# Two-layer decoder trunk: a fourth Strassen block in the first half of the second MLP product, and final results taken out of PSUM by ScalarE

## The chip, the core and the metric

The program runs on one core of a Trainium2 chip, in one launch. The time is the device time of one execution in microseconds; the kernel before takes 2175.74 us (median of 3 runs, 2175.13 to 2176.91). In the text TensorE is the matrix engine (PE in the rows, its weight loads PEld), VectorE is DVE, ScalarE is ACT, and SyncE (SP) issues most of the DMAs.

## The reference, cut to what matters

The input is 256 tokens of 2048 channels in float32. Layer 0 is a hybrid of a gated convolution and differential attention, layer 1 is forgetting attention; after each comes the part that the change touches, a dense MLP with 8192 hidden channels:

```
def _sqrelu_mlp(h, w1, w2):
    return jnp.square(jax.nn.relu(h @ w1)) @ w2

h = _rmsnorm(x, norm2_g[l])
x = x + _sqrelu_mlp(h, mlp_w1[l], mlp_w2[l])
```

The results must agree with float32 arithmetic. The kernel therefore writes each operand as the sum of a high and a low part in a reduced format (float32r), and each product as three: high by high, high by low, low by high.

## The kernel before, in words

**Splitting.** A weight tile of 1 MB comes in by one DMA on SP's queue (`raw`, 3 buffers). `split_w` (L139 to L148) makes its high part on ScalarE (`wh`, L146) and its low part on VectorE (`wl`, L147); of each there are 3 buffers in a ring, so a tile's cast waits until TensorE is done with the tile three back.

**Order.** A Tile scheduler sets the order in which instructions stand on each engine when the program is built, and adds semaphores. On the chip each engine goes through its queue in that order. `pending` holds generators of small work (attention, norm chunks), which `step` moves on by one piece after a block of matmuls; `late` holds closures that take a result out of PSUM, and `flush` runs them when the next product's first weights have been split.

**One MLP.** `mlp` (L700) goes through 4 groups of 2048 hidden channels. In each group `hidden` (L606) computes eight products of the first weight (`gemm_t`, two weight tiles each, 64 matmuls of 512 columns and 64 of 256), and `take` squares the result and splits it into a `PairS` or a `PairC` by the letter in `KINDS`. Then `gemm_pair` (L639) runs twice, for column blocks n = 0, 1 and n = 2, 3. It is called the first and the second pair here. Each has eight blocks, one for every letter of `KINDS`:

- A block C is eight products of three matmuls of 512 columns (24 matmuls), from one weight tile.
- A block S is Strassen's form with seven products (21 matmuls). VectorE makes four sums of weights first (`T`, L652 to L655), and two tiles are split: `wa` of 1536 columns from `raw`, and `wb` of 2048 from `T`. The first three products (P1, P2, Q3) need `wa`, the last four (Q5, P7, P6, Q4) `wb`.

A pair fills all eight PSUM banks. P1, Q5, P7 and P6 are only written by blocks S. After the block behind the last S they are combined into `E` and added to the residual `xall` (L680 to L689: one ScalarE copy, five VectorE instructions counted as L682, L683, L684 and twice L689). P2, Q3, X and Q4 collect up to the pair's last product, and `final` (L693) takes them out, with one VectorE instruction each that scales the bank and adds it to the residual (L695), when the next pair or the next group has started.

**The turn from layer 0 to layer 1.** In the last group `done` puts the norm chunks of the next layer on `pending`: chunks 0 and 1 behind `E` of the second pair, chunks 2 and 3 behind the last `final`. A chunk transposes a column block of the residual on TensorE (L198) and splits it into high (ScalarE, L135) and low (VectorE, L136). The first projection of layer 1 (`gemm`, L150) needs chunk 0 for its first matmuls.

The tiles `T`, `E` and the hidden blocks' results share the pool `qkv` under the name `qk`, with 2 buffers.

Of the kernel before, what the change touches and what calls it, by code (L numbers as in the profile page):

```python
# [8 lines left out]
F32 = mybir.dt.float32  # L9
F32R = mybir.dt.float32r  # L10
AF = mybir.ActivationFunctionType
# [5 lines left out]
P = 128  # L17
D = 2048
# [8 lines left out]
def trunk_kernel(  # L27
# [54 lines left out]


    pending = []
    late = []

    def flush():

        while late:
            late.pop(0)()  # L90

    def step():

# [56 lines left out]
    def gemm(acts, w, c0, first=False):  # L150

        acc = []
        total = 4 * len(acts)
        i = 0
        for ai, a in enumerate(acts):
            raw = wraw.tile([P, 4, CW], F32, name="raw")
            src = w[a.row:a.row + CW, c0:c0 + CW].rearrange("(k p) n -> p k n", p=P)
            if first and ai == 0:
                for h in range(4):
                    nc.sync.dma_start(raw[:, h, :], src[:, h, :])  # L160
            else:
                nc.sync.dma_start(raw, src)
            wh, wl = split_w(raw, parts=4 if first and ai == 0 else 2 if first else 1)
            if i == 0:
                flush()
# [76 lines left out]
    gw = const.tile([P, KT, 16], F32, name="gw")  # L242
    gws = const.tile([P, GP], F32R, name="gws")

    def setup():
        rows = work.tile([P, 2 * P], F32, name="y")[:, :P]
# [12 lines left out]
        nc.scalar.dma_start(gw, fox_w_in[0, :, 3 * D:3 * D + 16].rearrange("(k p) n -> p k n", p=P))  # L259


        nc.gpsimd.memset(mask, 0.0)
# [162 lines left out]

    def forget_gates(nm):

        wv = gws[:, :KT * 32].rearrange("p (k n) -> p k n", n=32)
        nc.scalar.copy(gws[:, KT * 32:], ones[:, :96])
        nc.scalar.copy(wv[:, :, 0:16], gw)  # L430
# [115 lines left out]
    def gemm_t(acts, w, c0):  # L546


        acc = []
        for c in range(2):  # L550
            raw = wraw.tile([P, 8, 2 * P], F32, name="raw")
            r0 = c * 8 * P
            nc.sync.dma_start(raw, w[r0:r0 + 8 * P, c0:c0 + 2 * P].rearrange("(k p) n -> p k n", p=P))
            wh, wl = split_w(raw, (8, 2 * P))
            if c == 0:
                flush()
                acc += [accp.tile([P, CW], F32, name="acc") for _ in range(2)]
            for h in range(2):
                a = acts[2 * c + h]
                until(lambda: a.left <= 0)  # L560
                for f, k, p in TORDER:
                    fs = slice(f * P, (f + 1) * P)
                    if p == 0:
                        nc.tensor.matmul(  # L564
                            acc[f], wh[:, 4 * h + k, fs], a.both[:, k, :, :].rearrange("p s t -> p (s t)"),
                            start=c + h + k == 0, stop=False)
                    else:
                        nc.tensor.matmul(acc[f][:, 2 * P:], wl[:, 4 * h + k, fs], a.hi[:, k, :], start=False,  # L568
                                         stop=(c, h, k) == (1, 1, 3))
                step()  # L570
        return acc

    KINDS = "SCSCSCCC"

    class PairS:

# [8 lines left out]
            nc.scalar.copy(self.t[:, :, 0, :], f)  # L587
            nc.vector.tensor_tensor(self.t[:, :, 1, :], f, self.t[:, :, 0, :].bitcast(F32), ALU.subtract)

        def part(self, i):  # L590
            return self.t[:, i, 0, :], self.t[:, i, 1, :]

    class PairC:
# [12 lines left out]
    def hidden(nm, w, c0):  # L606

        pairs, half = [], None
        for i, kind in enumerate(KINDS):
            acc = gemm_t(nm.acts, w, c0 + 2 * i * P)  # L610
            if kind == "S":
                p = PairS()
            elif half is not None:
                p, half = PairC(half), None
            elif "C" in KINDS[i + 1:]:
                t = actp.tile([P, 4, 2, 2 * P], F32R, name="act")
                p, half = PairC(t[:, :2]), t[:, 2:]
            else:
                p = PairC(qkv.tile([P, 2, 2, 2 * P], F32R, name="v"))
# [19 lines left out]
    def gemm_pair(pairs, w, r0, n, r2, done):  # L639

        B = {}
        live = set()
        for i, (kind, p) in enumerate(zip(KINDS, pairs)):
# [5 lines left out]
            more = KINDS[i + 1:]  # L649
            if kind == "S":  # L650
                T = qkv.tile([P, 4, CW], F32, name="qk")
                nc.vector.tensor_tensor(  # L652
# [3 lines left out]
                wa, wb = split_w(raw[:, 1:4]), split_w(T)  # L656
            else:
                wa = split_w(raw)
            if i == 0:
                flush()  # L660
# [14 lines left out]
            else:  # L675
                for k in range(2):
                    for bank, t, h in (("P2", 0, 1), ("Q3", 0, 0), ("X", 1, 0), ("Q4", 1, 1)):
                        mul(bank, p.part(k, t), wa, 2 * k + h, not more and k == 1)
            if i == KINDS.rindex("S") + 1:
                E = qkv.tile([P, 4, CW], F32, name="qk")  # L680
                nc.scalar.copy(E[:, 3], B["P1"])
                nc.vector.tensor_tensor(E[:, 2], B["P6"], E[:, 3], ALU.add)  # L682
                nc.vector.tensor_tensor(E[:, 1], B["P7"], E[:, 2], ALU.add)  # L683
                nc.vector.tensor_tensor(  # L684
                    E[:, 0:3:2], B["Q5"].unsqueeze(1).broadcast_to([P, 2, CW]), E[:, 1:3], ALU.subtract)
                for t in (1, 0):
                    x2 = xall[:, n:n + 2, t, :]
                    e = E[:, 2 - 2 * t:4 - 2 * t]
                    nc.vector.scalar_tensor_tensor(x2, e, r2[:, t:t + 1], x2, ALU.mult, ALU.add)  # L689
                done(0)  # L690
            step()

        def final():  # L693
            for bank, m, t in (("P2", n + 1, 0), ("Q3", n, 0), ("X", n, 1), ("Q4", n + 1, 1)):
                nc.vector.scalar_tensor_tensor(  # L695
                    xr[m][:, t, :], B[bank], r2[:, t:t + 1], xr[m][:, t, :], ALU.mult, ALU.add)
                done(1, m, t)
        late.append(final)

    def mlp(nm, l, nxt):  # L700
        ov = out[0].rearrange("(t p) d -> p t d", p=P)
        r2 = None
        for g in range(4):
# [5 lines left out]
            for n in (0, 2):  # L709
                def done(stage, m=None, t=None, n=n, g=g):  # L710
# [10 lines left out]
                gemm_pair(pairs, mlp_w2[l], g * D, n, r2, done)  # L721
        if nxt is None:
            flush()

    def load_x(n):
        if n > 0:
# [69 lines left out]
```

## Time and profile before

| what | value |
|---|---|
| median of 3 runs | 2175.74 us |
| profiled execution | 2178.49 us |
| its span, first to last instruction | 2176.8 us |
| TensorE busy, matmuls | 2166.2 us, 10738 records |
| TensorE weight loads busy | 1818.3 us |
| VectorE busy | 1547.4 us |
| ScalarE busy | 1052.7 us |
| DMA | 412.08 MB, 189 GB/s over the span |

The profiled execution lies 2.75 us above the median, and 1.7 us of its time lie outside the span. Busy time is a sum over the whole span; matmuls overlap in the pipeline, so TensorE's pace is read from the distance between the starts of matmuls and not from the busy time.

### The profile page before, as it was taken

Reading aid. Unit: us, or ns where it says so; the run is one execution under the profiler, and the core shown is the slowest. Engines: PE = TensorE matmul, PEld = TensorE weight load, DVE = VectorE, ACT = ScalarE, POOL = GpSimd, SP = SyncE. Lnnn points to the kernel's source line nnn. Section 1 sums busy time; section 2 is a strip of 40 time slices with the busy share of each in tenths; the row PEclk is TensorE's granted clock in tenths of the full one; section 3 lists DMA queues with packets and bytes.
Section 4 is the critical chain, followed back from the end, with each engine's and each line's share of the span. In section 5 each row is a group of like instructions: output and inputs, shape, how many; then the busy total and the mean of one; then the engine's idle time right before and its main releaser. Section 6 shows DMA issues by size and latency. Waiting matters only on the chain. (4 is left out here: it accounts for less than half of the span.)

```text
span 2176.8 us, 26071 instructions
## 1 busy us (share of the span) xinstructions
PE 2166.2 (100%) x10738; PEld 1818.3 (84%) x10738; DVE 1547.4 (71%) x1574; ACT 1052.7 (48%) x1101; POOL 19.1 (1%) x17
## 2 busy tenths in 40 slices
PE   9999999999999999999999999999999999999999
PEld 7887888888888888888888888888888888888887
DVE  5666655778769768767855565567787697687687
ACT  6455443544444444445554454445444444444453
POOL 0000000000000000000000000000000000000000
PEclk9999999999999999999999999999999999999999
DMA  8544556555665665665645555555566656656654
GB/s 272 180 159 158 187 177 200 178 167 198 220 193 170 220 193 182 211 189 190 210 163 194 187 183 173 185 166 176 168 207 216 193 174 216 190 191 207 186 192 151
DMA packets 245273, 412.08 MB, mean 189 GB/s; under 512 B 9399, under 2 KB 144802, under 8 KB 245154
## 3 DMA queue, kind: packets, MB, share of 16 engines
q1 hardware_dynamic: 237296, 405.84, 57.6%
q10 hardware_dynamic: 7858, 4.58, 0.7%
q8 instruction: 84, 1.38, 0.3%
q14 instruction: 35, 0.29, 0.0%
HBM read 408.28 MB, written 2.11 MB: 189 GB/s over the span
## 5 line engine op out<-in xcount | busy, mean ns | idle before, releaser
L147 DVE TENSOR_TENSOR wl<-raw,wh 128x2048 fp32r<-128x2048 f32 (+3 forms) x390 | 855.7, 2196 | 476.8 <-ACT wh L146 476.3
L146 ACT CAST wh<-raw 128x2048 fp32r<-128x2048 f32 (+3 forms) x390 | 713.6, 1832 | 654.3 <-PE acc L179 232.0
L564 PE MATMUL acc<-act,wh 128*128 128x512 f32 x2048 | 643.8, 396 | 0.0
L179 PE MATMUL acc<-wh,act 128*128 128x512 f32 x2048 | 565.0, 397 | 0.1
L568 PEld LDWEIGHTS acc<-act,wl 128*128 128x128 f32 x2048 | 384.7, 188 | 90.7
L179 PEld LDWEIGHTS acc<-wh,act 128*128 128x128 f32 x2048 | 376.5, 188 | 75.3 <-issue 2.0
L568 PE MATMUL acc<-act,wl 128*128 128x256 f32 x2048 | 402.4, 278 | 0.0
L179 PE MATMUL acc<-wl,act 128*128 128x512 f32 x1024 | 318.8, 391 | 0.3 <-DVE wl L147 0.3
L564 PEld LDWEIGHTS acc<-act,wh 128*128 128x128 f32 x2048 | 312.3, 189 | 0.8
L636 PE MATMUL acc<-wl,act 128*128 128x512 f32 x656 | 256.1, 390 | 2.1 <-DVE wl L147 1.9
L637 PE MATMUL acc<-wh,act 128*128 128x512 f32 x656 | 255.3, 389 | 0.0
L635 PE MATMUL acc<-wh,act 128*128 128x512 f32 x656 | 251.5, 389 | 0.0
L179 PEld LDWEIGHTS acc<-wl,act 128*128 128x128 f32 x1024 | 192.1, 188 | 42.8 <-issue 0.7
L636 PEld LDWEIGHTS acc<-wl,act 128*128 128x128 f32 x656 | 123.1, 188 | 30.7 <-DVE wl L147 5.2
L635 PEld LDWEIGHTS acc<-wh,act 128*128 128x128 f32 x656 | 123.1, 188 | 25.7
L637 PEld LDWEIGHTS acc<-wh,act 128*128 128x128 f32 x656 | 123.2, 188 | 25.3
L146 ACT CAST wh<-qk 128x2048 fp32r<-128x2048 f32 x48 | 91.8, 1913 | 92.9 <-DVE qk L655 68.7
L147 DVE TENSOR_TENSOR wl<-qk,wh 128x2048 fp32r<-128x2048 f32 x48 | 109.9, 2290 | 22.2 <-ACT wh L146 21.6
L626 ACT COPY qk<-acc 128x256 f32<-128x256 f32 x128 | 47.1, 368 | 132.4 <-PE acc L568 132.4
L635 PE MATMUL tp<-wh,act 128*128 128x512 f32 x192 | 74.7, 389 | 0.0
L636 PE MATMUL tp<-wl,act 128*128 128x512 f32 x192 | 74.7, 389 | 0.0
L637 PE MATMUL tp<-wh,act 128*128 128x512 f32 x192 | 74.7, 389 | 0.0
(173 smaller groups left out, 1434.4 us busy)
## 6 DMA issues: line engine op xcount, KB each, us to landing
raw<-in_mlp_w_dram SPq DMA_DIRECT2D x256, 1024.0 KB, 5.5
raw<-in_fox_w_in_dram SPq DMA_DIRECT2D x48, 1024.0 KB, 5.2
raw<-in_hyb_w_in_dram SPq DMA_DIRECT2D x47, 1024.0 KB, 5.2
raw<-in_hyb_w_out_dram SPq DMA_DIRECT2D x16, 1024.0 KB, 5.2
raw<-in_fox_w_out_dram SPq DMA_DIRECT2D x16, 1024.0 KB, 5.1
ob<-fcd ACTq DMA_DIRECT2D x4, 512.0 KB, 4.5
xr<-in_x_dram SPq DMA_DIRECT2D x3, 512.0 KB, 7.4
raw<-in_hyb_w_in_dram SPq DMA_DIRECT2D x4, 256.0 KB, 4.5
```

The lines of the kernel that those rows point to most:

```text
L146: nc.scalar.copy(wh[:, s], src[:, s])
L147: nc.vector.tensor_tensor(wl[:, s], src[:, s], wh[:, s].bitcast(F32), ALU.subtract)
L179: nc.tensor.matmul(acc[t], x, (wl if p == 1 else wh)[:, k, :], start=st, stop=sp)
L564: nc.tensor.matmul(acc[f], wh[:, 4 * h + k, fs], a.both[:, k, :, :].rearrange("p s t -> p (s t)"), start=c + h + k == 0, stop=False)
L568: nc.tensor.matmul(acc[f][:, 2 * P:], wl[:, 4 * h + k, fs], a.hi[:, k, :], start=False, stop=(c, h, k) == (1, 1, 3))
L626: nc.scalar.copy(fj, acc[j][:, 2 * P:])
L635: nc.tensor.matmul(acc, a[0], b[0], start=not started, stop=False)
L636: nc.tensor.matmul(acc, a[0], b[1], start=False, stop=False)
L637: nc.tensor.matmul(acc, a[1], b[0], start=False, stop=last)
```

## The change

- `KINDS` now holds a row of letters for each pair. The first pair (n = 0) goes from S C S C S C C C to S C S S C S C C, the second (n = 2) to S C S C C S C C. The hidden block with index 3 is stored as a `PairS`, and in the second pair it is used as a C, by way of `part(k, t)`.
- `E` is now combined at `kinds.rindex("S") + 2`, the last block of a pair, behind the split of that block's weights and ahead of its products; before, it stood behind the products of the block with index `rindex("S") + 1`.
- `final` now has two halves. ScalarE takes the four banks into a tile `F` of the `qk` ring, scaled (L713); a single VectorE addition of 2048 columns (L717) adds `F` to the residual. The addition waits in a second list, `later`, and is flushed when the second weight tile of what follows has been split. The last pair of layer 1 keeps the old form (`tail`).
- The small weight of the forget gates (`gw`) and its split (`gws`) lose their own buffers. `gw` is loaded in `forget_gates`, into a tile `y`, and the split goes into a tile of the `act` ring.

The core of the diff:

```diff
-    KINDS = "SCSCSCCC"
+    KINDS = {0: "SCSSCSCC", 2: "SCSCCSCC"}
...
-        def part(self, i):
+        def part(self, i, t=None):
+            i = i if t is None else 2 * i + t
             return self.t[:, i, 0, :], self.t[:, i, 1, :]
...
-            elif "C" in KINDS[i + 1:]:
+            elif i < 3:
                 t = actp.tile([P, 4, 2, 2 * P], F32R, name="act")
                 p, half = PairC(t[:, :2]), t[:, 2:]
             else:
                 p = PairC(qkv.tile([P, 2, 2, 2 * P], F32R, name="v"))
...
-            if i == KINDS.rindex("S") + 1:
+            if i == 1:
+                flush(later)
+            if i == kinds.rindex("S") + 2:
                 E = qkv.tile([P, 4, CW], F32, name="qk")
                 nc.scalar.copy(E[:, 3], B["P1"])
...
                 done(0)
+            if i == 0:
+                flush(late)
...
         def final():
-            for bank, m, t in (("P2", n + 1, 0), ("Q3", n, 0), ("X", n, 1), ("Q4", n + 1, 1)):
-                nc.vector.scalar_tensor_tensor(
-                    xr[m][:, t, :], B[bank], r2[:, t:t + 1], xr[m][:, t, :], ALU.mult, ALU.add)
-                done(1, m, t)
+            if tail:
...
+                return
+            F = qkv.tile([P, 4, CW], F32, name="qk")
+            for bank, j in (("P2", 2), ("Q3", 0), ("X", 1), ("Q4", 3)):
+                nc.scalar.activation(F[:, j], B[bank], AF.Copy, scale=r2[:, j % 2:j % 2 + 1])
+
+            def add():
+                x4 = xall[:, n:n + 2].rearrange("p m t n -> p (m t) n")
+                nc.vector.tensor_tensor(x4, x4, F, ALU.add)
+                for j in range(4):
+                    done(1, n + j // 2, j % 2)
+            later.append(add)
         late.append(final)
...
     def forget_gates(nm):
 
+        gt = actp.tile([P, 16 * P], F32R, name="act")
+        gws = gt[:, :GP]
+        gw = work.tile([P, 2 * P], F32, name="y").rearrange("p (k n) -> p k n", n=16)
+        nc.scalar.dma_start(gw, fox_w_in[0, :, 3 * D:3 * D + 16].rearrange("(k p) n -> p k n", p=P))
+        yield
```

In the order listings below a row is one instruction (or several equal ones): its line, operation, output tile and inputs, and the output's shape. Line numbers of the changed kernel are higher: the weight sums L652, L654, L655 are L661, L663, L664 there; `E` is L673, L674, L675 and L680; the products L635 to L637 are L643 to L645.

VectorE where the second pair starts, before. The first row is the last bank of `E`; the rows L695 are the old `final`.

```order
L684 TENSOR_TENSOR qk<-tp,qk 128x2x512
L652 TENSOR_TENSOR qk<-raw 128x1024
L689 SCALAR_TENSOR_TENSOR xr<-qk,r_3711,xr 128x2x512 x2
L654 TENSOR_TENSOR qk<-qk,raw 128x512
L147 TENSOR_TENSOR wl<-raw,wh 128x1536
L655 TENSOR_TENSOR qk<-qk,raw 128x512
L652 TENSOR_TENSOR qk<-raw 128x1024
L654 TENSOR_TENSOR qk<-qk,raw 128x512
L695 SCALAR_TENSOR_TENSOR xr<-acc,r_3711,xr 128x512
L147 TENSOR_TENSOR wl<-qk,wh 128x2048
L695 SCALAR_TENSOR_TENSOR xr<-acc,r_3711,xr 128x512 x3
L147 TENSOR_TENSOR wl<-raw,wh 128x2048
```

And now:

```order
L147 TENSOR_TENSOR wl<-raw,wh 128x2048
L673 TENSOR_TENSOR qk<-tp,qk 128x512
L147 TENSOR_TENSOR wl<-raw,wh 128x2048
L674 TENSOR_TENSOR qk<-tp,qk 128x512
L661 TENSOR_TENSOR qk<-raw 128x1024
L675 TENSOR_TENSOR qk<-tp,qk 128x2x512
L663 TENSOR_TENSOR qk<-qk,raw 128x512
L680 SCALAR_TENSOR_TENSOR xr<-qk,r_3712,xr 128x2x512 x2
L664 TENSOR_TENSOR qk<-qk,raw 128x512
L147 TENSOR_TENSOR wl<-raw,wh 128x1536
L147 TENSOR_TENSOR wl<-qk,wh 128x2048
L717 TENSOR_TENSOR xr<-xr,qk 128x2048
```

The first row now is the low part for the first pair's block with index 6, and the second L147 that for index 7. All of `E` stands between these and the second pair's first weights, and behind L717 comes the low part for the second pair's block with index 1.

ScalarE at the same place, before: the high parts for index 7 of the first pair and 0 of the second, and then on.

```order
L681 COPY qk<-tp 128x512
L146 CAST wh<-raw 128x2048 x2
L146 CAST wh<-raw 128x1536
L146 CAST wh<-qk 128x2048
L146 CAST wh<-raw 128x2048
```

And now:

```order
L672 COPY qk<-tp 128x512
L146 CAST wh<-raw 128x2048
L146 CAST wh<-raw 128x1536
L713 ACTIVATE qk<-acc,r_3712 128x512
L146 CAST wh<-qk 128x2048
L713 ACTIVATE qk<-acc,r_3712 128x512 x3
L146 CAST wh<-raw 128x2048
L146 CAST wh<-raw 128x1536
```

The first bank is taken out ahead of the high part of the second pair's `T`, the other three ahead of the high part for index 1.

TensorE in the second pair now, from the first matmul that uses the weights of index 1 (wh_5312, wl_5313). Five matmuls need only high parts, the sixth is the first that needs the low part; wh_5347 belongs to index 2.

```order
L643 MATMUL acc_5281<-wh_5312,act_4448 128x512
L643 MATMUL acc_5282<-wh_5312,act_4448 128x512
L643 MATMUL acc_5284<-wh_5312,act_4448 128x512
L643 MATMUL acc_5283<-wh_5312,act_4448 128x512
L643 MATMUL tp_5285<-wh_5347,act_4535 128x512
L644 MATMUL acc_5281<-wl_5313,act_4448 128x512
L645 MATMUL acc_5281<-wh_5312,act_4448 128x512
```

The scheduler draws high-by-high matmuls forward in the same way inside index 0 (four of them, ahead of the first that needs the low part of `T`) and in index 2.

VectorE at the turn to layer 1, before. L136 are low parts of the next layer's norm chunks.

```order
L684 TENSOR_TENSOR qk<-tp,qk 128x2x512
L689 SCALAR_TENSOR_TENSOR xr<-qk,r_3711,xr 128x2x512 x2
L136 SCALAR_TENSOR_TENSOR act<-tp,g_95,act 128x256 x2
L147 TENSOR_TENSOR wl<-raw,wh 128x2048 x2
L136 SCALAR_TENSOR_TENSOR act<-tp,g_95,act 128x256 x2
L695 SCALAR_TENSOR_TENSOR xr<-acc,r_3711,xr 128x512 x4
L147 TENSOR_TENSOR wl<-raw,wh 128x2048
L136 SCALAR_TENSOR_TENSOR act<-tp,g_95,act 128x256 x4
```

And now:

```order
L675 TENSOR_TENSOR qk<-tp,qk 128x2x512
L680 SCALAR_TENSOR_TENSOR xr<-qk,r_3712,xr 128x2x512 x2
L147 TENSOR_TENSOR wl<-raw,wh 128x2048
L717 TENSOR_TENSOR xr<-xr,qk 128x2048
L136 SCALAR_TENSOR_TENSOR act<-tp,g_95,act 128x256 x4
L147 TENSOR_TENSOR wl<-raw,wh 128x2048
```

Before, the four low parts of chunk 0 stood ahead of the last results (L695); now they stand behind the addition L717, which needs those results.

## Rows read from the trace of the kernel before

**Rows 1.** The page: busy time of the engines; TensorE's granted clock in 40 slices

```profile
PE 2166.2 (100%) x10738; PEld 1818.3 (84%) x10738; DVE 1547.4 (71%) x1574; ACT 1052.7 (48%) x1101; POOL 19.1 (1%) x17
...
PEclk9999999999999999999999999999999999999999
```

**Rows 2.** Timeline, TensorE in group 2's pairs: start, duration, instruction

```profile
871.32 0.39 PE L635 MATMUL tp<-wh,act 128*128 128x512 f32 x1
...
896.50 0.39 PE L635 MATMUL acc<-wh,act 128*128 128x512 f32 x1
...
901.94 0.39 PE L635 MATMUL acc<-wh,act 128*128 128x512 f32 x1
```

**Rows 3.** Groups of instructions: count, busy us, mean ns, idle before

```profile
L637 PEld LDWEIGHTS acc<-wh,act 128*128 128x128 f32 x656 | 123.2, 188 | 25.3
```

**Rows 4.** Busy time in two stretches: eight hidden blocks, then the first pair

```profile
747.00:829.32 82.32, 82.32 (x475) 71.84 (x474) 56.46 (x57) 36.80 (x38) 0.00 (x0) 1.00 0.63 189
829.32:871.30 41.98, 41.77 (x185) 34.27 (x184) 36.98 (x31) 20.94 (x14) 0.00 (x0) 1.00 0.58 191
```

**Rows 5.** Waits of TensorE's weight loads for `wl`: us in total, times, longest

```profile
PEld acc L636 <- DVE wl L147: 5.2, 8, 1.8
```

**Rows 6.** Timeline, TensorE: one of these waits, at index 3 of group 2's first pair

```profile
844.29 0.39 PE L635 MATMUL acc<-wh,act 128*128 128x512 f32 x1
844.89 0.50 PE L636 MATMUL acc<-wl,act 128*128 128x512 f32 x1 [0.21 <-DVE wl L147]
```

**Rows 7.** Timeline, VectorE, from the first pair's last S into the second pair

```profile
852.38 2.29 DVE L147 TENSOR_TENSOR wl<-raw,wh 128x2048 fp32r<-128x2048 f32 x1 [3.61 <-ACT wh L146]
854.59 0.69 DVE L682 TENSOR_TENSOR qk<-tp,qk 128x512 f32<-128x512 f32 x1
855.20 2.28 DVE L147 TENSOR_TENSOR wl<-raw,wh 128x2048 fp32r<-128x2048 f32 x1
...
860.20 1.22 DVE L684 TENSOR_TENSOR qk<-tp,qk 128x1024 f32<-128x1024 f32 x1
861.33 1.21 DVE L652 TENSOR_TENSOR qk<-raw 128x1024 f32<-128x1024 f32 x1
862.46 2.47 DVE L689 SCALAR_TENSOR_TENSOR xr<-qk,r,xr 128x1024 f32<-128x1024 f32 x2
864.85 0.68 DVE L654 TENSOR_TENSOR qk<-qk,raw 128x512 f32<-128x512 f32 x1
865.46 1.75 DVE L147 TENSOR_TENSOR wl<-raw,wh 128x1536 fp32r<-128x1536 f32 x1
867.12 0.68 DVE L655 TENSOR_TENSOR qk<-qk,raw 128x512 f32<-128x512 f32 x1
867.73 1.22 DVE L652 TENSOR_TENSOR qk<-raw 128x1024 f32<-128x1024 f32 x1
...
874.42 2.28 DVE L147 TENSOR_TENSOR wl<-raw,wh 128x2048 fp32r<-128x2048 f32 x1
```

**Rows 8.** Timeline, ScalarE: a cast released by VectorE, and one by TensorE

```profile
867.92 1.91 ACT L146 CAST wh<-qk 128x2048 fp32r<-128x2048 f32 x1 [5.79 <-DVE qk L655]
...
902.14 1.92 ACT L146 CAST wh<-raw 128x2048 fp32r<-128x2048 f32 x1 [3.52 <-PE acc L637]
```

**Rows 9.** Groups by shape: a PSUM bank taken by ScalarE, and by VectorE

```profile
L229 ACT ACTIVATE qk<-acc,rstd 128x512 f32<-128x512 f32 x32 | 20.7, 683 | 0.9 <-PE acc L179 0.9
...
L695 DVE SCALAR_TENSOR_TENSOR xr<-acc,r,xr 128x512 f32<-128x512 f32 x64 | 44.3, 743 | 5.5 <-PE acc L637 5.5
```

**Rows 10.** Timeline at the turn from layer 0 to layer 1, VectorE and TensorE

```profile
1084.79 0.87 DVE L136 SCALAR_TENSOR_TENSOR act<-tp,g,act 128x256 fp32r<-128x256 f32 x2
1085.58 2.72 DVE L695 SCALAR_TENSOR_TENSOR xr<-acc,r,xr 128x512 f32<-128x512 f32 x4
...
1086.38 0.60 PE L198 MATMUL tp<-ident,xr 128*128 128x128 f32 x4
1086.73 0.48 PE L179 MATMUL acc<-wh,act 128*128 128x512 f32 x1
```

More of the change, by code (lines that the diff above doesn't have):

```diff
@@ L84, in trunk_kernel, with flush @@
     pending = []
[L85 to L90, printed above, removed]
+    late, later = [], []
+    def flush(held):
+        while held:
+            held.pop(0)()
     def step():
@@ L163, in gemm @@
             wh, wl = split_w(raw, parts=4 if first and ai == 0 else 2 if first else 1)
-            if i == 0:
-                flush()
+            if i > 0:
+                flush(later)
+            else:
+                flush(late)
                 acc += [accp.tile([P, CW], F32, name="acc") for _ in range(2)]
@@ L241, in trunk_kernel @@
     GP = 16 * 32 + 96
-    gw = const.tile([P, KT, 16], F32, name="gw")
-    gws = const.tile([P, GP], F32R, name="gws")
     def setup():
@@ L258, in setup @@
         nc.scalar.dma_start(bfb, fox_b_f.broadcast_to([P, 16]))
-        nc.scalar.dma_start(gw, fox_w_in[0, :, 3 * D:3 * D + 16].rearrange("(k p) n -> p k n", p=P))
         nc.gpsimd.memset(mask, 0.0)
@@ L554, in gemm_t @@
             wh, wl = split_w(raw, (8, 2 * P))
-            if c == 0:
-                flush()
+            if c > 0:
+                flush(later)
+            else:
+                flush(late)
                 acc += [accp.tile([P, CW], F32, name="acc") for _ in range(2)]
@@ L608, in hidden @@
         pairs, half = [], None
-        for i, kind in enumerate(KINDS):
+        for i, kind in enumerate(KINDS[0]):
             acc = gemm_t(nm.acts, w, c0 + 2 * i * P)
@@ L637, in products, with gemm_pair @@
         nc.tensor.matmul(acc, a[1], b[0], start=False, stop=last)
-    def gemm_pair(pairs, w, r0, n, r2, done):
+    def gemm_pair(pairs, w, r0, n, r2, done, tail):
         B = {}
         live = set()
-        for i, (kind, p) in enumerate(zip(KINDS, pairs)):
+        kinds = KINDS[n]
+        for i, (kind, p) in enumerate(zip(kinds, pairs)):
             raw = wraw.tile([P, 4, CW], F32, name="raw")
@@ L647, in gemm_pair @@
                 w[r0 + 2 * i * P:r0 + 2 * (i + 1) * P, n * CW:(n + 2) * CW].rearrange("(k p) n -> p k n", p=P))
-            more = KINDS[i + 1:]
+            more = kinds[i + 1:]
             if kind == "S":
@@ L658, in gemm_pair @@
                 wa = split_w(raw)
+            if i == 1:
+                flush(later)
+            if i == kinds.rindex("S") + 2:
+                E = qkv.tile([P, 4, CW], F32, name="qk")
+                nc.scalar.copy(E[:, 3], B["P1"])
+                nc.vector.tensor_tensor(E[:, 2], B["P6"], E[:, 3], ALU.add)
+                nc.vector.tensor_tensor(E[:, 1], B["P7"], E[:, 2], ALU.add)
+                nc.vector.tensor_tensor(
+                    E[:, 0:3:2], B["Q5"].unsqueeze(1).broadcast_to([P, 2, CW]), E[:, 1:3], ALU.subtract)
+                for t in (1, 0):
+                    x2 = xall[:, n:n + 2, t, :]
+                    e = E[:, 2 - 2 * t:4 - 2 * t]
+                    nc.vector.scalar_tensor_tensor(x2, e, r2[:, t:t + 1], x2, ALU.mult, ALU.add)
+                done(0)
             if i == 0:
-                flush()
+                flush(late)
                 for nm in ("P2", "Q3", "Q4", "X"):
@@ L678, in gemm_pair @@
                         mul(bank, p.part(k, t), wa, 2 * k + h, not more and k == 1)
-            if i == KINDS.rindex("S") + 1:
[L680 to L690, printed above, removed]
             step()
         def final():
-            for bank, m, t in (("P2", n + 1, 0), ("Q3", n, 0), ("X", n, 1), ("Q4", n + 1, 1)):
-                nc.vector.scalar_tensor_tensor(
-                    xr[m][:, t, :], B[bank], r2[:, t:t + 1], xr[m][:, t, :], ALU.mult, ALU.add)
-                done(1, m, t)
+            if tail:
+                for bank, m, t in (("P2", n + 1, 0), ("Q3", n, 0), ("X", n, 1), ("Q4", n + 1, 1)):
+                    nc.vector.scalar_tensor_tensor(
+                        xr[m][:, t, :], B[bank], r2[:, t:t + 1], xr[m][:, t, :], ALU.mult, ALU.add)
+                    done(1, m, t)
+                return
[8 more added lines that the diff above has]
+            later.append(add)
         late.append(final)
@@ L720, in done @@
                         pending.extend([nxt.chunk(2), nxt.chunk(3)])
-                gemm_pair(pairs, mlp_w2[l], g * D, n, r2, done)
+                gemm_pair(pairs, mlp_w2[l], g * D, n, r2, done, nxt is None and g == 3 and n == 2)
         if nxt is None:
-            flush()
+            flush(late)
     def load_x(n):
```

## The prediction

> **What bounds the kernel now.** I read the busy times first: TensorE's matmuls fill the span, and its clock is at the full level, 2.4 GHz, in all 40 slices [rows 1]. Busy time can hide slack, so the pace comes from the timeline. The 24 matmuls of one block C take 901.94 - 896.50 = 5.44 us, 0.2267 us each [rows 2]; a block S, with 21, takes 4.76. Inside blocks the starts are that far apart without a hole, so every matmul taken away is worth 0.227 us, unless TensorE then waits.
>
> *A rule read against this.* The Trainium skill ("Perfetto Trace Analysis", Identifying the Most-Contended Engine) judges TensorE's headroom by the share of weight loads and not by matmul busy time, since matmuls overlap. Weight loads fill 84% here [rows 1], which would leave a sixth free, and fewer matmuls would then bring nothing. But a load takes 188 ns [rows 3] of a pitch of 227, so 83% is what a gapless stretch shows; by the trace there is no headroom. By the rule the sum below would be 5.4 us higher.
>
> The windows say which engine is next. While eight hidden blocks run, VectorE works 56.5 of 82.3 us; in a pair 37.0 of 42.0 [rows 4]. A pair has little room, and less than the average says: the split buffers let a weight tile be cast only when TensorE has left the one three back, so VectorE can't work ahead. The waits confirm it: TensorE's only repeated waits in the pairs are eight for a low part, 5.2 us by their weight loads [rows 5]. They stand at index 3 of each group's first pair. One of them moved the next matmul from 0.23 to 0.60 us behind [rows 6]; I count 0.5 us each, 4 us in all. At the second pair's start TensorE doesn't wait at all: P1 starts at 871.32 [rows 2], and its low part began at 865.46 [rows 7].
>
> **What it removes.** One C of 24 matmuls becomes an S of 21 in each of the 8 first pairs (2 layers, 4 groups): 24 matmuls x 0.2267 = 5.4 us. The four waits per layer at index 3 I also take as gone, -4 us: an S asks for `T` there only with its fourth product, and VectorE's order at that place is another. Bounds: -5.2 and 0 (they come back in another form).
>
> **What it adds to VectorE in the first pair.** By starts that follow back to back [rows 7], an S costs VectorE 1.13 (L652) + 2 x 0.61 (L654, L655) + 1.66 + 2.2 = 6.2 us, against 4.76 of TensorE; a C costs 2.2 against 5.44. So each S that replaces a C takes 4 us of VectorE's room, gives 0.68 less cover, and `E` (0.61 + 0.61 + 1.13 + 2.39 = 4.75) moves behind the last S, with two blocks C after it instead of three. 4 x 6.2 + 4 x 2.2 + 4.75 + 2.2 (L717) = 40.6 against 4 x 4.76 + 4 x 5.44 = 40.8: full, with no room for a hand-over. What that costs depends on where the queue is late, so I walk it.
>
> **The walk at the second pair's start.** Time 0 is the pair's first matmul if TensorE had not waited; index 7 began at -5.44, index 6 at -10.88, index 5 (the last S) at -15.64. Hand-overs: a cast starts 0.2 us behind the block that frees its buffer (902.14 against 901.94), VectorE to ScalarE 0.1 (867.80 to 867.92) [rows 2, 7, 8]; ScalarE to VectorE and VectorE to TensorE I take at 0.05, an estimate below the smallest of these.
> - The cast for index 6 waits for the buffer of index 4, free at -15.64: it runs to -13.5 (1.91), and `wl` follows, 2.2, to -11.3.
> - By then P6 of index 5 has landed too (-15.64 + 6 x 0.68 + 0.2 = -11.4), so `E` starts, and VectorE works without a pause in the order shown: L673 0.61, `wl` of index 7 2.2, L674 0.61, L661 1.13, L675 1.13, L663 0.61, L680 2.39 (to -2.6), L664 0.61 (to -2.0), `wl` of `wa` 1.66, to -0.3. P1's second matmul needs this at 0.23: just in time. Before, the same `wl` began 5.9 us ahead of the pair.
> - ScalarE: the first L713 needs `E`'s buffer (free at -2.6) and P2's last product (-2.04 + 0.2), so it runs from -1.8 to -1.2. L713 is the operation of L229, 0.68 us [rows 9], 0.6 back to back. Then the cast of `T`, to 0.7; VectorE makes its low part to 3.05. TensorE has done P1, P2, Q3 (2.04) and four high-by-high matmuls (0.91) at 2.95: wait 0.15.
> - Then L717. No row has it; by elements it is two L652 (2.4), by operation and size the `wl` of 2048 columns (2.2 back to back) [rows 7]. I take 2.2; the least is 1.1 (half, as if it ran two elements at a time), the most 2.5. It ends at 5.2, and `wl` of index 1 stands behind it: 7.5. TensorE ends index 0 at 4.9 and has five high-by-high matmuls (1.13) to 6.05. Wait 1.5 us. This is the largest one; its price falls one for one with L717's.
> - Behind this `wl` come L661, the 1536 `wl`, L663 and L664 (1.13 + 1.66 + 1.22 = 4.0, to 11.5), the cast of `T` of index 2 (to 13.5) and only then the cast for index 3 (to 15.4). TensorE comes to index 3's first drawn-forward matmul at 7.55 + 20 x 0.227 (index 1) + 8 x 0.227 + 0.91 = 14.8. Wait 0.6.
> From there two blocks C in a row (index 3 and 4) give VectorE 2 x (5.44 - 2.2) = 6.5 us back. I add 0.15 for index 3 of the first pair, where the low part of `T` is ready within a tenth or two of its need. Sum 2.4 per group, x 8 = 19 us. Bounds: with L717 at 1.1 it is 1.2 per group, 10 us; with hand-overs 0.05 longer at each of the some ten steps, 3 per group, 24.
>
> *A rule on the evictions.* Four banks taken by ScalarE cost it 4 x 0.68; VectorE paid 4 x 0.74 [rows 9]. The Trainium skill ("VectorE: DVE Perf Modes", Specifications) says that ScalarE sits closer to PSUM and VectorE closer to SBUF, which speaks for this move. The trace has 683 against 743 ns, hardly a difference; VectorE saves 3.0 per pair and pays 2.2 back, and by the rule nothing in the walk changes.
>
> **The turn to layer 1.** Before, chunk 0 was split before the MLP ended, and layer 1 starts 1086.73 right behind the transposes [rows 10]. Now its four L136 stand behind L717, and L717 behind the last eviction. From the MLP's end: last eviction to 0.2 + 0.68 = 0.9, L717 to 3.2, the first two L136 (0.4 each [rows 10]) to 4.0. Meanwhile TensorE has eight transposes (four span 0.6 with the tail of the last [rows 10]; some 0.9 us) and two high-by-high matmuls, to 1.4. Its wait is 2.4 for the first low part, and I add 1 for chunk 1, whose L136 stand behind the next `wl`. 3.4 us, once; bounds 0 and 5.
>
> **At no cost.** `PairS` for `PairC` at index 3 of the hidden blocks: 1.5 us of VectorE and 0.4 of ScalarE per group, covered by the 26 us that VectorE is idle there [rows 4]. L717 behind the second pair stands in the hidden blocks too, with the same cover. `gw`: 128 KB once, its DMA stands far ahead in ScalarE's queue, in layer 0's output projection; the tile from the `act` ring is the ninth of nine and delays no split. If either cover fails: one split, under 2 us.
>
> **Sum.** -5.4 - 4 + 19 + 3.4 = +13. The profiled execution took 2178.5 (span 2176.8), so a profiled one should take 2191.5; the median lies 2.75 lower: 2175.7 + 13 = **2189 us**.
>
> **Rivals.**
> - *The matmuls decide (faster).* If VectorE is 1.5 us earlier at the second pair's start, the low part of index 1 is there in time and only -5.4 to -9.4 remain: 2166 to 2170. For it speaks that TensorE has not one wait at that place before. Against it: VectorE's `wl` began 5.9 us ahead then, and one block C of 5.44 and nothing else was its cover. It decides from a VectorE queue shorter by 1.5 us of 17; the rows repeat to some hundredths. 0.07.
> - *Half the wait (no change).* L717 at 1.1 us, or the drawn-forward matmuls cover more: 10 us of waits, no wait at the turn, -9.4: 2176, within 0.2% (4.4 us, about what a measurement of this kernel can tell from no change). 0.10.
> - *It runs away (slower).* The first pair is full by the sum above; if each hand-over is longer, index 5 and the second pair's `T` wait too: 24 + 5 - 5.4 = +24, 2199. 0.13.
> - *The forecast*, 2181 to 2196: 0.70.
>
> The range should hold 8 in 10: 2176 to 2200. Slower by over 0.2% is the forecast and the last rival, 0.83; within 0.2% 0.10; faster 0.07.
>
> **What will show it.** 24 fewer matmul records. In the waits: TensorE for L147 some 14 us in 16 or more waits and for L146 some 5 in 8, all in second pairs; a wait of about 1.5 us right behind L717 eight times; at the turn one of 2 to 3 us for L136. VectorE in a pair near 41 of 43 us. Index 3 of the first pair without its wait of 0.5. L717 at 2.2 to 2.3 us. The forecast is wrong if TensorE starts index 1 of the second pair without a wait; then L717 or the chain ahead of it is cheaper than its rows.

## The result, and the profile after

The changed kernel takes **2193.72 us** (median of 4 runs, 2192.57 to 2194.68); the kernel before took 2176.28 beside it. The ratio is 1.0078, 95% interval 1.0065 to 1.0090. The prediction said slower, 2189, with a range of 2176 to 2200. The profiled execution took 2193.47 (span 2191.8), 15.0 us more than the profiled one of before, which lay 2.2 us above its median. The ratios in this document leave out two far slower executions, one of the kernel before (2380.08 us) and the profiled one of run 7 (4398.76), so that run 7 has times only.

The page, busy times and granted clock, beside [rows 1]:

```profile
PE 2168.1 (99%) x10714; PEld 1809.7 (83%) x10714; DVE 1580.2 (72%) x1585; ACT 1101.6 (50%) x1169; POOL 18.4 (1%) x17
...
PEclk9999999999999999999999999999999999999999
```

24 matmul records are gone, and VectorE and ScalarE have 33 and 49 us more work. The clock is at its full level in every slice, so the loss is waiting. The waits of TensorE in the second product, beside [rows 5] (us in total, times, longest):

```profile
PEld acc L644 <- DVE wl L147: 12.6, 8, 1.6
...
PE acc L644 <- DVE wl L147: 9.3, 8, 1.2
...
PEld acc L643 <- ACT wh L146: 6.4, 8, 0.8
PEld tp L644 <- DVE wl L147: 5.0, 16, 0.6
```

Before, there were eight waits of 5.2 us by the weight loads. Now there are 24 for low parts and eight for a cast. The timeline of TensorE shows where they stand in group 2, whose second pair starts at 872.56 (start, us, line; in brackets the idle time and its releaser):

```profile
872.56 0.39 PE L643 MATMUL tp<-wh,act 128*128 128x512 f32 x1
...
880.04 0.50 PE L644 MATMUL acc<-wl,act 128*128 128x512 f32 x1 [1.16 <-DVE wl L147]
888.00 0.96 PE L643 MATMUL acc<-wh,act 128*128 128x512 f32 x3 [0.37 <-ACT wh L146]
```

Measured by the starts against the pitch of 0.227, these two cost 1.43 us at index 1 and 0.64 at index 3 of the second pair, in each of the eight groups. Three holes of about 0.1 (index 3 of the first pair, the start of index 0) make 0.3 more, so 2.4 per group; starts that lie less than 0.06 us late add some 0.2. VectorE on the way there, which answers to [rows 7]:

```profile
856.13 2.29 DVE L147 TENSOR_TENSOR wl<-qk,wh 128x2048 fp32r<-128x2048 f32 x1 [2.05 <-ACT wh L146]
859.11 2.29 DVE L147 TENSOR_TENSOR wl<-raw,wh 128x2048 fp32r<-128x2048 f32 x1 [0.69 <-ACT wh L146]
...
865.86 1.21 DVE L675 TENSOR_TENSOR qk<-tp,qk 128x1024 f32<-128x1024 f32 x1
866.99 0.68 DVE L663 TENSOR_TENSOR qk<-qk,raw 128x512 f32<-128x512 f32 x1
867.59 2.47 DVE L680 SCALAR_TENSOR_TENSOR xr<-qk,r,xr 128x1024 f32<-128x1024 f32 x2
869.98 0.68 DVE L664 TENSOR_TENSOR qk<-qk,raw 128x512 f32<-128x512 f32 x1
870.59 1.75 DVE L147 TENSOR_TENSOR wl<-raw,wh 128x1536 fp32r<-128x1536 f32 x1
873.29 2.29 DVE L147 TENSOR_TENSOR wl<-qk,wh 128x2048 fp32r<-128x2048 f32 x1 [0.96 <-ACT wh L146]
875.50 2.29 DVE L717 TENSOR_TENSOR xr<-xr,qk 128x2048 f32<-128x2048 f32 x1
877.70 2.29 DVE L147 TENSOR_TENSOR wl<-raw,wh 128x2048 fp32r<-128x2048 f32 x1
```

The two new operations, grouped by shape (busy us, mean ns):

```profile
L713 ACT ACTIVATE qk<-acc,r 128x512 f32<-128x512 f32 x60 | 39.3, 689 | 69.6 <-PE acc L645 69.6
L717 DVE TENSOR_TENSOR xr<-xr,qk 128x2048 f32<-128x2048 f32 x15 | 34.3, 2288 | 4.4 <-ACT qk L713 4.4
```

So both cost what the rows of before gave them [rows 7, 9]. The low part of index 0's sums begins at 873.29, 0.7 us behind the pair's first matmul, and L717 follows. The low part that index 1 needs comes third and ends at about 880.0, when TensorE goes on. The windows, first and second pair of that group (beside [rows 4]: length; then busy time and count of PE, PEld, DVE, ACT, POOL; granted clock, DMA share, GB/s):

```profile
831.56:872.56 41.00, 41.00 (x183) 33.72 (x181) 37.46 (x31) 22.32 (x16) 0.00 (x0) 1.00 0.52 180
872.56:916.47 43.91, 42.38 (x185) 33.99 (x184) 37.30 (x24) 24.40 (x19) 0.00 (x0) 1.00 0.66 216
```

Without waits they would take 40.8 and 41.5 us. TensorE's loss is in the second window, although VectorE is no busier there than in the first. What counts is how late VectorE enters it.

The 15.0 us by place: I add the lengths of the pairs, from the first matmul's start to one pitch behind the last one's. Before it is 669.0 us for all eight groups, now 679.6. Without any wait it would be 16 pairs of 41.49 = 663.8 before, and 658.3 with the 24 matmuls gone; so what lies above that went from 5.2 to 21.3. (0.9 of the 5.2 are no waits: eight transposes of layer 1's chunks, 0.11 each, stood inside the last pair of layer 0.) The other 4.4 us lie outside the pairs, 4.0 of them at the turn to layer 1 (from the last pair of layer 0 to the first of layer 1: 489.7 against 485.7 us). Of these 4.0, 0.9 are the eight transposes, which now stand behind the pair, 2.2 are the waits below, by the starts, and the rest lies further on in layer 1. This answers to [rows 10]:

```profile
1090.38 0.39 PE L645 MATMUL acc<-wh,v 128*128 128x512 f32 x1
1090.62 1.03 PE L200 MATMUL tp<-ident,xr 128*128 128x128 f32 x8
1091.92 0.73 PE L181 MATMUL acc<-wh,act 128*128 128x512 f32 x2 [0.27 <-ACT act L135]
1094.27 0.73 PE L181 MATMUL acc<-wh,act 128*128 128x512 f32 x2 [1.62 <-DVE act L136]
```

```profile
1088.62 2.28 DVE L147 TENSOR_TENSOR wl<-raw,wh 128x2048 fp32r<-128x2048 f32 x1
1091.53 2.29 DVE L717 TENSOR_TENSOR xr<-xr,qk 128x2048 f32<-128x2048 f32 x1 [0.63 <-ACT qk L713]
1093.74 1.65 DVE L136 SCALAR_TENSOR_TENSOR act<-tp,g,act 128x256 fp32r<-128x256 f32 x4
```

All eight transposes of chunks 0 and 1 stand behind the MLP's last matmul, and their four L136 behind L717.

### The profile page after: what moved, and what is told of

The parts are those of the page before. It is cut to its first block, busy times and chain, and to the rows that moved or that the text cites. A ratio compares the mean times of both kernels' runs of the same rounds, so it can differ in the third digit from the quotient of the medians.

```text
span 2191.8 us, 26099 instructions
## 1 busy us (share of the span) xinstructions
PE 2168.1 (99%) x10714; PEld 1809.7 (83%) x10714; DVE 1580.2 (72%) x1585; ACT 1101.6 (50%) x1169; POOL 18.4 (1%) x17
## 4 chain that ended last, share of the span: by engine, by line
PE 93%; DVE 3%; ACT 2%; DMA 1%; issue 1%; ACTq 0%; SPq 0%; DVEq 0%
PE acc L181 31%; PE acc L570 22%; PE acc L574 11%; PE acc L644 7%; PE acc L645 7%; PE acc L643 7%; DVE wl L147 2%; PE tp L644 2%; PE tp L645 2%; PE tp L643 2%; ACT wh L146 2%; DVE xr L717 1%; DMA xr<-in_x_dram 0%; PE tp L318 0%; PE tp L200 0%
## 5 line engine op out<-in xcount | busy, mean ns | idle before, releaser
L147 DVE TENSOR_TENSOR wl<-raw,wh 128x2048 fp32r<-128x2048 f32 (+3 forms) x390 | 851.8, 2186 | 426.6 <-ACT wh L146 426.2
L146 ACT CAST wh<-raw 128x2048 fp32r<-128x2048 f32 (+3 forms) x390 | 709.0, 1824 | 542.4 <-PE acc L181 238.7
L181 PE MATMUL acc<-wh,act 128*128 128x512 f32 x2048 | 565.9, 397 | 2.5 <-DVE act L136 1.6
L181 PEld LDWEIGHTS acc<-wh,act 128*128 128x128 f32 x2048 | 375.6, 188 | 79.3 <-DVE act L136 3.3
L181 PE MATMUL acc<-wl,act 128*128 128x512 f32 x1024 | 318.7, 391 | 0.1
L181 PEld LDWEIGHTS acc<-wl,act 128*128 128x128 f32 x1024 | 192.1, 188 | 42.9 <-issue 0.7
L644 PE MATMUL acc<-wl,act 128*128 128x512 f32 x488 | 191.1, 392 | 9.3 <-DVE wl L147 9.3
L645 PE MATMUL acc<-wh,act 128*128 128x512 f32 x488 | 190.2, 390 | 0.0
L643 PE MATMUL acc<-wh,act 128*128 128x512 f32 x488 | 185.1, 393 | 3.0 <-ACT wh L146 3.0
L147 DVE TENSOR_TENSOR wl<-qk,wh 128x2048 fp32r<-128x2048 f32 x56 | 128.3, 2291 | 72.0 <-ACT wh L146 71.2
L146 ACT CAST wh<-qk 128x2048 fp32r<-128x2048 f32 x56 | 107.0, 1911 | 142.5 <-DVE qk L664 121.1
L644 PEld LDWEIGHTS acc<-wl,act 128*128 128x128 f32 x488 | 91.6, 188 | 32.2 <-DVE wl L147 12.6
L643 PEld LDWEIGHTS acc<-wh,act 128*128 128x128 f32 x488 | 91.0, 188 | 26.6 <-ACT wh L146 6.4
L645 PEld LDWEIGHTS acc<-wh,act 128*128 128x128 f32 x488 | 91.6, 188 | 18.6
L645 PE MATMUL acc<-wh,v 128*128 128x512 f32 x256 | 99.6, 389 | 0.0
L643 PE MATMUL acc<-wh,v 128*128 128x512 f32 x256 | 99.6, 389 | 0.0
L644 PE MATMUL acc<-wl,v 128*128 128x512 f32 x256 | 99.6, 389 | 0.0
```

Source lines behind the costliest of these rows:

```text
L146: nc.scalar.copy(wh[:, s], src[:, s])
L147: nc.vector.tensor_tensor(wl[:, s], src[:, s], wh[:, s].bitcast(F32), ALU.subtract)
L643: nc.tensor.matmul(acc, a[0], b[0], start=not started, stop=False)
```

## The experiments

Three theories stood against each other: the fourth S fills VectorE's queue ahead of a second pair that starts with an S; the evictions by ScalarE with L717 make the wait (rival A); E one block later makes it (rival B). Each run was timed beside the kernel before. All numbers in one table (the medians of before lay between 2176.3 and 2177.1 beside the runs; each ratio is against the one beside it): "pairs" is the sum of the lengths of the eight groups' pairs, "turn" the stretch between the layers, both of the profiled execution.

| kernel | median us | ratio to before, 95% | span | pairs | turn |
|---|---|---|---|---|---|
| before | 2176.5 | | 2176.8 | 669.0 | 485.7 |
| changed | 2193.7 | 1.0065 to 1.0090 | 2191.8 | 679.6 | 489.7 |
| fourth S alone | 2193.6 | 1.0063 to 1.0092 | 2191.9 | 675.1 | 486.9 |
| eviction alone | 2181.9 | 1.0014 to 1.0031 | 2180.3 | 672.3 | 486.1 |
| E later alone | 2178.4 | 1.0000 to 1.0018 | 2176.6 | 667.1 | 487.5 |
| second pair starts with C | 2174.4 | 0.9981 to 0.9999 | 2172.3 | 660.7 | 489.7 |
| addition on GpSimd | 2222.9 | 1.0194 to 1.0222 | 2221.1 | 707.5 | 491.6 |
| no addition at the turn | 2192.7 | 1.0058 to 1.0083 | 2191.4 | 679.9 | 489.1 |
| C first, E early | 2172.0 | 0.9969 to 0.9987 | | | |
| C first, E early, no addition at the turn | 2171.7 | 0.9967 to 0.9986 | 2169.7 | 660.8 | 486.9 |
| addition left out | 2186.6 | 1.0033 to 1.0059 | 2186.5 | 673.4 | 491.3 |
| E early | 2190.9 | 1.0051 to 1.0078 | 2188.9 | 680.1 | 487.2 |

**1. The fourth S alone.** Against the changed kernel, E and `final` as before:

```diff
-            if i == kinds.rindex("S") + 2:      # ahead of the products
+            if i == kinds.rindex("S") + 1:      # behind them
...
-            if tail:
+            if True:
```

> The changed kernel with E back at its place behind the products of the block after the last S, and all final results added by VectorE straight from PSUM; what is left of the change is the fourth S in the first pair. Theory (the fourth S fills VectorE's queue in the first pair, and the second pair begins with an S that wants a sum and two low parts at once): most of the loss stays without the eviction and without the later E: 2184 to 2196, with TensorE's waits again in the first blocks of each second pair. Rival A (the eviction by ScalarE and the addition L717 in front of index 1 make the wait): without them the 24 matmuls decide, 2166 to 2172. Rival B (E one block later makes it): also 2166 to 2172 here.

2193.6: a loss of the same size is there without the eviction and with E at its old place. Rivals A and B, by which nothing of it was to be left, fall as the only cause. But it is spent elsewhere: the pairs lose 6.1 us and not 10.6, the turn 1.2, and 7.7 lie between the groups, where a wait appears that neither kernel has, of both layers' hidden blocks for the VectorE evictions, six times:

```profile
PE acc L570 <- DVE xr L707: 6.3, 6, 1.3
```

VectorE enters the next hidden blocks late as well. So the evictions by ScalarE do buy something (these six waits), and the longer pairs give it back.

At the second pair's start, by the starts, index 0, 1 and 3 cost 0.5, 0.5 and 0.7 us per group here, against 0.2, 1.4 and 0.6 in the changed kernel. The place is not free without L717: the old `final` stands there, 2.7 us of it ahead of index 1's low part (the last row), where L717 took 2.2.

```profile
873.55 0.74 DVE L707 SCALAR_TENSOR_TENSOR xr<-acc,r,xr 128x512 f32<-128x512 f32 x1
874.22 2.28 DVE L147 TENSOR_TENSOR wl<-qk,wh 128x2048 fp32r<-128x2048 f32 x1
876.41 2.06 DVE L707 SCALAR_TENSOR_TENSOR xr<-acc,r,xr 128x512 f32<-128x512 f32 x3
878.39 2.28 DVE L147 TENSOR_TENSOR wl<-raw,wh 128x2048 fp32r<-128x2048 f32 x1
```

So the run shows a loss with either form of the eviction. What the place would cost without any work of `final` it does not show.

**2. The eviction alone.** The kernel before, with the new `final` and the list `later` only.

> The kernel before (three S in both pairs, E at its old place), with only the evictions by ScalarE and the addition L717 of the change. Theory: the first pair leaves VectorE some 4 us per group more than with four S, so L717 costs at most 0.5 us per group, and the turn to layer 1 3 us: 2178 to 2184. Rival A (eviction and L717 make the wait): 1.3 to 1.9 us per group and the turn, +14 to +18: 2188 to 2195. Rival B: 2176 to 2180.

+5.4, as the theory had it: with three S, the pairs lose 0.4 us per group and the turn moves by 0.4. In two groups TensorE waits 0.76 and 0.41 us besides, which was not looked into.

**3. E later alone.** The kernel before, with E one block later, ahead of that block's products.

> The kernel before, with only E moved: its instructions are issued one block later, in front of that block's products. Three S in both pairs, final results on VectorE. Theory: no wait in the second pair's start; 2174 to 2179, with 1 to 2 us at the turn to layer 1 at most. Rival A: 2174 to 2177. Rival B (E one block later makes the wait): 1.3 us per group or more, 2186 or more.

+1.8 by the medians, the interval ends at no change. The pairs do not lengthen (667.1); the turn does, by 1.8, 0.4 of them four transposes that left the last pair. Rival B is wrong for the pairs and has a point at the turn.

**4. The second pair starts with a C.** The whole change, one string different:

```diff
-    KINDS = {0: "SCSSCSCC", 2: "SCSCCSCC"}
+    KINDS = {0: "SCSSCSCC", 2: "CCSSCSCC"}
```

> The changed kernel, whole, but the second pair takes its hidden blocks as C, C, S, S, C, S, C, C: it still has three S, and the first pair four (index 1 and 2 of the hidden blocks and the buffers are as before). So its first block needs no sum T and one low part instead of two, and the first S comes two blocks later. Theory: the waits of the second pair go (21 us less), the 24 matmuls show, and the turn to layer 1 keeps its 4 us: 2166 to 2175. Rival A: L717 still stands in front of index 1's low part, so 1.3 us per group stay: 2182 to 2190. Rival C (VectorE's sum of work in a group is what decides, wherever it lies): the sum is unchanged, 2190 to 2196.

2174.4, 19 us less than the changed kernel by one swap of blocks (index 0 and 3 of the second pair). Matmuls, sums, evictions and VectorE's busy time (1580.8 us) are the same, so rival C falls; L717 is there too, so rival A does. With runs 2 and 3, which have three S and lose at most 0.4 us per group in the pairs, it says that the loss needs both: four S in the first pair and an S at the second one's start. The pairs take 660.7, 2.4 above the sum without waits. VectorE there:

```profile
859.46 2.28 DVE L147 TENSOR_TENSOR wl<-raw,wh 128x2048 fp32r<-128x2048 f32 x1
...
862.91 2.48 DVE L680 SCALAR_TENSOR_TENSOR xr<-qk,r,xr 128x1024 f32<-128x1024 f32 x2
865.30 2.29 DVE L147 TENSOR_TENSOR wl<-raw,wh 128x2048 fp32r<-128x2048 f32 x1
867.50 1.22 DVE L661 TENSOR_TENSOR qk<-raw 128x1024 f32<-128x1024 f32 x1
868.64 2.28 DVE L717 TENSOR_TENSOR xr<-xr,qk 128x2048 f32<-128x2048 f32 x1
```

The second pair starts at 867.29. The low part of index 0 (859.46) is done 5.6 us before that; the one of index 1 (865.30) ends 0.3 us into the pair, 5 us ahead of its need, and L717 delays nobody.

**5. The addition on GpSimd.**

```diff
-                nc.vector.tensor_tensor(x4, x4, F, ALU.add)
+                (nc.vector if turn else nc.gpsimd).tensor_tensor(x4, x4, F, ALU.add)   # turn: g == 3
```

> The changed kernel, with the addition L717 given to GpSimd instead of VectorE, except in the last group of each layer (so the turn to layer 1 is as in the changed kernel). Theory as the prediction had it (the wait at index 1 falls one for one with what stands in front of its low part on VectorE): with VectorE 2.3 us earlier the wait of 1.43 us at index 1 goes in the 6 groups concerned, and of the 0.64 at index 3 most: -9 to -12, 2182 to 2185. Rival D (the wait at index 1 is set by the chain of T and by E ahead of it, as the run with the fourth S alone suggests, where L717 is missing and the total is the same): less than half of it goes, 2189 to 2193. Rival E (GpSimd's addition slows VectorE beside it, or holds the buffer F so long that a later T waits): no gain or worse, 2193 to 2205.

In the last group of each layer the addition stays on VectorE. 29 us worse than the changed kernel: rival E, and more than it allowed. GpSimd's and VectorE's timelines in group 2:

```profile
884.62 4.91 POOL L717 TENSOR_TENSOR xr<-xr,qk 128x2048 f32<-128x2048 f32 x1 [127.11 <-ACT qk L713]
```

```profile
885.10 5.51 DVE L661 TENSOR_TENSOR qk<-raw 128x1024 f32<-128x1024 f32 x1
890.54 2.28 DVE L147 TENSOR_TENSOR wl<-raw,wh 128x2048 fp32r<-128x2048 f32 x1
```

L661, 1.22 us elsewhere, stands for 5.51: it ends 1.1 us, about its own length, behind GpSimd's addition at 889.53. So it is in all six groups; behind their second pairs it is a low part, L147, that stands for 5.02 to 5.08 us instead of 2.29 and ends 2.15 behind GpSimd's addition. TensorE's wait at index 1 grows to 4.66 us beyond the pitch. The run says nothing on rival D.

The Trainium skill ("SBUF — State Buffer", SBUF: two separate sides) says that VectorE and GpSimd share a pair of SBUF ports as an exclusive lock for a whole instruction, when VectorE's reads two SBUF inputs. The trace agrees in what it can show: L661 reads two slices of `raw`, starts 0.5 us behind GpSimd's addition and ends about its own length behind it, and so does L147 with `raw` and `wh`.

**6. No addition at the turn.** The changed kernel, with `tail` for the last pair of layer 0 too.

> The changed kernel, but the last pair of layer 0 adds its final results by VectorE straight from PSUM, as the kernel before did (no L717 there); E keeps its later place. The waits in the pairs are as in the changed kernel; only the turn to layer 1 differs, where the period from layer 0's last group to layer 1's first is 4.1 us longer outside the pairs than before. Prediction's reason (L136 stands behind L717): all of it goes, 2189 to 2190. Theory now (E later and L717 each give a part, since E alone gave 1.8 there, the eviction with L717 alone 0.4, both 4): 1.8 stays, 2191 to 2192.

Only 1.0 us comes back by the medians, and 0.7 at the turn. TensorE now waits for ScalarE there, whose cast L146 stands ahead of L135:

```profile
1090.68 1.03 PE L200 MATMUL tp<-ident,xr 128*128 128x128 f32 x8
1093.21 1.25 PE L181 MATMUL acc<-wh,act 128*128 128x512 f32 x4 [1.49 <-ACT act L135]
```

**7 and 8. C first, E early; and without the addition at the turn.** The edits of 4 and of 1's first part; then also that of 6.

> The changed kernel with two edits: the second pair takes its blocks as C, C, S, S, C, S, C, C, and E is back at its old place in both pairs. The evictions by ScalarE and L717 stay everywhere. Theory: the pairs keep 82.5 us, the turn falls from +4 to about +0.4 since chunks 0 and 1 of the next layer are split a block earlier: 2168 to 2172. Rival (the earlier E makes VectorE wait for TensorE in the full first pair, and TensorE waits later for it): 2174 to 2180.

> As the run with C first and E early, and in addition the last pair of layer 0 adds its final results by VectorE straight from PSUM (no L717 at the turn). Theory: what the turn still costs goes too: 2166 to 2170, faster than both kernels. Rival (four additions from PSUM hold the banks longer than four evictions by ScalarE do, and layer 1's first products wait for them): no gain over the run without this edit, 2169 to 2173.

2172.0 and 2171.7: both beat both kernels, 0.2% below the kernel before. E at its old place gives 2.4 us over run 4. The last edit's 0.3 is within the spread, so L717 at the turn costs nothing that can be measured here.

**9. The addition left out.** Run 5 left the question of L717's price open. The addition is left out in the first three groups of each layer, so this kernel leaves their final results out of the output.

```diff
+                if turn:                                        # g == 3
                     nc.vector.tensor_tensor(x4, x4, F, ALU.add)
```

> The changed kernel, with the addition L717 left out in the first three groups of each layer (so those groups' final results are not added to the output; ScalarE's four evictions stay). Nothing takes its place on GpSimd, so the run with GpSimd's addition is repeated here without GpSimd. Prediction's reason (the wait at index 1 falls one for one with L717): all 1.43 us at index 1 go in 6 groups, 2185 or less. Theory now (ScalarE is next: its cast for index 1 ends at 876.5 us in group 2, where VectorE without L717 would be free at 875.5): the low part comes 1.1 us earlier and not 2.2, so 0.3 of the wait stays at index 1, and the 0.6 at index 3 stays: 6 x 1.1 = 6.6 us less, 2186 to 2188. Rival D (the chain of T and E sets it and L717 nothing): 2191 to 2194.

2186.6, as the theory had it in sum, but not in its parts: index 1 keeps 1.06 to 1.09 of its 1.43 us, and the wait at index 3 goes whole. VectorE there:

```profile
870.79 2.29 DVE L147 TENSOR_TENSOR wl<-qk,wh 128x2048 fp32r<-128x2048 f32 x1 [0.96 <-ACT wh L146]
873.00 1.22 DVE L661 TENSOR_TENSOR qk<-raw 128x1024 f32<-128x1024 f32 x1
874.25 0.69 DVE L663 TENSOR_TENSOR qk<-qk,raw 128x512 f32<-128x512 f32 x1
874.86 2.28 DVE L147 TENSOR_TENSOR wl<-raw,wh 128x2048 fp32r<-128x2048 f32 x1
```

The order has changed with the edit: two sums for index 2 now stand ahead of index 1's low part. So taking out the 2.2 us of L717 wins 1.0 us per group, and most of the wait at index 1 is there without it. In the old order, too, a part would have stayed. ScalarE in the changed kernel:

```profile
874.30 0.70 ACT L713 ACTIVATE qk<-acc,r 128x512 f32<-128x512 f32 x1
874.87 1.93 ACT L146 CAST wh<-raw 128x2048 fp32r<-128x2048 f32 x1
```

The cast for index 1 stands behind L713 and ends at 876.80 (the expectation has 876.5). The low part begins at 877.70; without L717 it could begin 0.9 us earlier at most, so an estimated 0.5 of the 1.43 stays. The turn's 491.3 in the table holds a stretch at the lower clock (last section).

**10. E early.** The changed kernel with 1's first edit only.

> The changed kernel with only one part undone: E is back at its old place, behind the products of the block after the last S. Fourth S, evictions by ScalarE and L717 stay. Theory now (the turn to layer 1 costs 4 us because E, one block later, brings the transposes and L136 of chunks 0 and 1 to the MLP's end): the turn falls to +0.4, 3.6 us less; the pairs keep their length within 0.6 us: 2186 to 2192. Prediction's reason (L136 stands behind L717 at the turn): L717 is still there, so the turn keeps its 4 us, and only the pairs can move: 2192 to 2196.

2190.9: the turn falls by 2.5 us with L717 in place, and the pairs stay (85.0 per group). 0.4 of the 2.5 are four transposes that stand inside the last pair again. The theory now holds for the direction at the turn, not for all of the 3.6.

## Why the prediction was right, and where it was not

- **The matmuls' price** (-5.4 us) holds: where the waits are gone, in run 4, the pairs take 658.3 + 2.4.
- **The waits at index 3 of the first pair** (-4): 0.11 each is left (0.47 in one group), as allowed for with 0.15.
- **The walk at the second pair's start** (2.4 per group, 19 us): 0.2, 1.43 and 0.64 us at index 0, 1 and 3 against 0.15, 1.5 and 0.6. VectorE's and ScalarE's order, with the 0.96 us that VectorE stands for the cast of `T`, is the one that was walked.
- **The reason given for the largest wait failed in its price.** "Its price falls one for one with L717's": run 9 took out 2.2 us and won 1.0. The step left out ScalarE, whose cast for index 1 is the next to be late: it lets the low part begin at most 0.9 us earlier. Run 9 does not price L717 alone either, since VectorE's order changed with it. Run 1 shows a loss of the same size with no L717 at all, though with the old `final` in its place. The cause is the sequence of blocks: a first pair with four S and a second one that begins with an S put `E`, two low parts and the sums of index 0 into one stretch of VectorE's queue (runs 1 and 4). L717 is one entry of that stretch.
- **The turn** (+3.4; 4.0 measured, 0.9 of them transposes that only moved) was near in size, by luck in part, and wrong in reason: "their four L136 stand behind L717". The wait is there, 1.62 us, but without L717 only 0.7 of the 4.0 goes, since TensorE then waits 1.49 us for ScalarE (run 6); with E early and L717 in place 2.5 goes (run 10). (By its own terms the first wait is 4.0 - 1.4 = 2.6, where 2.4 was added.) E one block later brings the transposes to the MLP's end; what they then wait for, L717 or a cast, matters little. Each part alone moved the turn by 1.2, 0.4 and 1.8 us (runs 1 to 3).
- **The sum**: +13 was forecast; 15.0 lie between the two profiled executions (-5.4, waits in the pairs 16.1 where 15 were summed, 4.4 outside them where 3.4 were). The median was 4.7 us above the forecast. 2 us of this are the sum's; the rest comes from the profiled execution of before, which lay over 2 us above its median where that of after did not: the forecast took the offset along.
- **VectorE's busy time** in a pair was to be near 41 of 43 us; it is 37.5 of 41.0 in the first and 37.3 of 43.9 in the second. The pair is not full. Late in the first VectorE stands 2.05 and 0.69 us for casts (at 856.13 and 859.11 in the timeline above), and enters the second pair late all the same: a busy share below one was no room.
- **The rival "the matmuls decide"** named VectorE 1.5 us earlier as its condition. Run 4 more than makes it so, and gets the gain that the rival described, less the turn.

What stays open: why the six waits of run 1 and the longer pairs of the changed kernel sum to the same time within 0.1 us. It may be chance.

## What to carry to other kernels

When an edit trades the bounding engine's work for work of the next one, ask in which stretch of that engine's queue the new work lies and what has to be ready right behind it; the same work, two blocks later, was worth 19 us here. Undo the parts of a change one at a time before a wait is put down to the instruction that stands in front of it: three parts were suspected, and the one with no new instruction at the waiting place carried most of the loss.

## What was not expected of the hardware

GpSimd's addition held VectorE for 4.3 us six times, and for 2.8 us six times more (run 5). The wait that followed also changed TensorE's clock. The windows around it, and the starts:

```profile
885.00:888.00 3.00, 3.00 (x15) 2.37 (x13) 2.97 (x2) 2.65 (x2) 3.00 (x1) 1.00 0.43 169
888.00:892.80 4.80, 0.37 (x2) 0.00 (x0) 4.80 (x3) 0.00 (x0) 1.52 (x1) 1.00 0.00 0
892.80:897.00 4.20, 4.13 (x11) 3.29 (x12) 2.89 (x4) 1.20 (x1) 0.00 (x0) 0.59 0.69 232
```

```profile
894.27 0.63 PE L644 MATMUL acc<-wl,act 128*128 128x512 f32 x1
894.70 0.63 PE L645 MATMUL acc<-wh,act 128*128 128x512 f32 x1
...
897.09 0.40 PE L643 MATMUL acc<-wh,act 128*128 128x512 f32 x1
897.33 0.40 PE L644 MATMUL acc<-wl,act 128*128 128x512 f32 x1
```

TensorE stood for 4.7 us; then the granted clock averages 0.59, and matmuls start 0.43 us apart, the pitch at the lower level (1.2 GHz), until 896.8, when 0.23 returns. In four of the six groups eight or nine matmuls take some 0.2 us more, in the other two fourteen: 1.7 to 3.0 us on top of the wait. In the changed kernel, neither the 1.43 us at index 1 nor the 1.9 us at the turn did that: the granted clock of the profiled execution stays at 1.00. But behind the same wait at the turn it did fall in runs 5 and 9; of run 9, the window behind it:

```profile
1091.00:1094.20 3.20, 3.20 (x9) 2.45 (x9) 2.97 (x3) 2.56 (x9) 0.00 (x0) 0.51 0.22 83
```

Run 9's profiled execution has a mean clock of 0.999. So have two of the four executions of the changed kernel, 2193.98 and 2194.68 us, while the other two, 2193.47 and 2192.57, have 1.000. The fall thus seems to come in some executions of a kernel and not in others; where it stood in those two no trace shows, and what decides it no run here tells.
